# Where the sums of weight blocks are made: an accumulating DMA against VectorE and GpSimd, in a decoder trunk of seven-product matmuls

## The chip, the cores and the metric

One Trainium2 chip, one core. The metric is the device time of one execution in microseconds. DVE is VectorE, ACT ScalarE, PE TensorE (PEld its weight loads), POOL GpSimd and SP the engine that issues most of the DMAs.

## The reference

A decoder trunk of two layers on 1024 tokens of width 1024, all in float32. Layer 1 is a gated short convolution and a SwiGLU feed-forward block (FFN, hidden width 2816); layer 2 is latent attention with 8 heads and another FFN; a norm closes it.

```python
def short_conv_mixer(h, w_in, conv_w, w_out):
    u = h @ w_in                                   # 1024 -> 3 x 1024
    gate_b, gate_c, val = jnp.split(u, 3, axis=-1)
    z = gate_c * val
    conv = sum(conv_w[k] * zp[:, k:k + s] for k in range(3))   # zp: z shifted by up to 2 tokens
    return (gate_b * conv) @ w_out

def swiglu_ffn(h, w13, w2):
    g, u = jnp.split(h @ w13, 2, axis=-1)          # 1024 -> 2 x 2816
    return (jax.nn.silu(g) * u) @ w2

for i in range(2):
    h = h + (short_conv_mixer if i == 0 else mla_mixer)(rms_norm(h), ...)
    h = h + swiglu_ffn(rms_norm(h), w13[i], w2[i])
return rms_norm(h)
```

## The kernel before

**Three matmuls for one.** Every operand of a large matmul is split into a high part in the matmul's own format (`hi`, a cast on ScalarE, line 112) and the rest (`lo`, a subtraction on VectorE, line 113); `three` (lines 153 to 155) multiplies hi by hi, lo by hi and hi by lo into one bank of PSUM.

**Seven products for eight.** The matmuls into the gated layers (the `up` stages) take two blocks of 128 output columns at a time, a *quad*: the columns `ca` and `cb` of the weight, each cut into a top and a bottom half along the contraction (a0, a1, b0, b1). Instead of eight products of quarter size, seven are made, in the order 1, 2, 5, 6, 7, 4, 3. Products 1 and 2 use a0 and a1 as they are (`pair`, one split of 128x1024); 4 uses b1; 5 uses b0+b1, 6 uses a0+b0+b1, 7 uses a0+b0 and 3 uses a0+a1+b0+b1 (`half(i)`, a split of 128x512 each). One product is 12 matmuls of 128x512. `evict` adds the bank of a product into the results C1 and C2 on VectorE, in part through ScalarE, and the functions in `done` follow the last product.

**The sums.** A quad's weights lie in two tiles of 128x1024, `ra` and `rb`, from a pool of 5 buffers (`raw_tile`, named `wr` in the profile). `load` (line 363) fetches them on SP's queue. The sums are made in the tile by the DMA itself: `plus` (line 378) issues from GpSimd's queue a DMA of 256 KB that fetches a block from memory and adds it to what the tile holds. There are four per quad.

**Stages.** In order: `up` of the convolution (12 quads; three quads make two column pairs, gate_c with val, and the pair of gates for both), `Plain` (the product with w_out), `up` of FFN 1 (22 quads), `Down` of FFN 1, the latents and attention, `Plain` for the attention's output, `up` of FFN 2 (22 quads), `Down` of FFN 2 and the output. `Down` has seven products too, with weight sums of its own: `weight_sums` (line 884) has GpSimd issue DMAs, half of them from memory to memory with an addition, that leave these sums in `md["f1w"]` and `md["f2w"]` in memory. It does so during the `up` stage of the same FFN.

**The order is written out by hand.** `Steps` holds a list of TensorE steps (a product is one step); `before(n, f)` and `after(n, f)` put work ahead of step n and behind it. The program is issued in that order, so each engine's queue is in order of steps. `up` (line 446) gives the order: of the first 7 quads (FILL) products 1 and 2 come first, 14 steps; then the other five products of the first two quads in turn, then five products each of quads 2 to 6; the remaining quads run all seven. In these 49 steps products 5, 6, 7, 4 and 3 need operands that are still being prepared in the first 14 (`Operand.second`). A quad is loaded 9 or 12 steps ahead of its product 5; a `half` stands 2 steps (4 for product 5) ahead of its product.

Of the kernel before, what the change touches and what calls it, by code (L numbers as in the profile page):

```python
# [12 lines left out]
AF = mybir.ActivationFunctionType  # L13
ALU = mybir.AluOpType
AX = mybir.AxisListType

P = 128
S = 1024
D = 1024
KD = D // P  # L20
DFF = 2816
# [28 lines left out]
def trunk(ctx, tc, aps, out):  # L50
    nc = tc.nc
    A = aps
# [115 lines left out]
    for nm in ("conv_norm_g", "conv_w", "conv_ffn_norm_g", "kv_norm_g", "mla_norm_g", "kv_latent_norm_g",  # L168
               "mla_q_norm_g", "mla_ffn_norm_g", "final_norm_g"):
        a = A[nm]  # L170
        if len(a.shape) == 3:
            a = a.rearrange("a b c -> (a b c)")
        elif len(a.shape) == 2:
            a = a.rearrange("a b -> (a b)")
        n = a.shape[0] // P
# [64 lines left out]
    class Stream:  # L240


        def __init__(self):
            self.h = [None] * KD
            self.acc = None

    st = Stream()
    hd = dram.tile([KD, P, S], F32, name="hd")
    md = {"conv": dram.tile([KD, P, S], F32, name="md_conv")}
# [32 lines left out]
    class Operand:  # L282
# [16 lines left out]
        def part(self, name, kk, b):  # L299

            hi, lo = slot("xh", F32R), slot("xl", F32R)
            nc.scalar.copy(out=hi, in_=b)
            self.late.append(lambda: nc.vector.tensor_tensor(lo, b, hi.bitcast(F32), ALU.subtract))  # L303
            self.X.setdefault(name, {})[kk] = (hi, lo)
# [46 lines left out]
    class Quad:  # L351


        def __init__(self, wv, ca, cb, first, done):
            self.wv, self.ca, self.cb, self.first, self.done = wv, ca, cb, first, done
            self.W, self.bank = {}, {}

        def part(self, c, p):
            return self.wv[:, 4 * p:4 * p + 4, c:c + P]

        def load(self, c, n=8):
            r = raw_tile("wr")
            nc.sync.dma_start(r[:, :n * P].rearrange("p (k m) -> p k m", m=P), self.wv[:, :n, c:c + P])
            return r

        def load_a(self):
            self.ra = self.load(self.ca)

        def load_top(self):

            self.ra = self.load(self.ca, 4)

        def load_b(self):
            self.rb = self.load(self.cb)

        def plus(self, r, c, p):

            nc.gpsimd.dma_start(r[:, :512].rearrange("p (k m) -> p k m", m=P), self.part(c, p), accum_op=ALU.add)  # L378

        def pair(self):  # L380
            hi, lo = hi_tile("w_hi"), lo_tile("w_lo")
            split(hi, lo, self.ra)
            self.W[1], self.W[2] = (hi, lo, 0), (hi, lo, 512)

        def half(self, i):

# [55 lines left out]
    def up(steps, quads, op):  # L442

        head, n0 = quads[:FILL], len(steps.pe)
        a, b = quads[:2]
        n = {}

        for x, i in [(a, 1), (b, 1), (a, 2), (b, 2), *((x, i) for x in head[2:] for i in (1, 2)),
                     *((x, i) for i in (5, 6, 7, 4, 3) for x in (a, b)),
                     *((x, i) for x in quads[2:] for i in ((5, 6, 7, 4, 3) if x in head else (1, 2, 5, 6, 7, 4, 3)))]:  # L450
            n[x, i] = x.add(steps, op, i)
        for x in head:
            steps.before(n[x, 1] - 9, x.load_a)
            steps.before(n[x, 1] - 2, x.pair)
        for x in quads:
            n5 = n[x, 5]
            if x in head:
                steps.before(n5 - 9, x.load_top, x.load_b)
            else:
                steps.before(n5 - 12, x.load_a, x.load_b)  # L460
                steps.before(n5 - 5, x.pair)
            steps.before(n5 - 7, lambda x=x: x.plus(x.rb, x.cb, 1))
            steps.before(n5 - 4, lambda x=x: x.half(5))
            steps.before(n5 - 4, lambda x=x: x.plus(x.ra, x.cb, 0))
            steps.before(n5 - 3, lambda x=x: x.plus(x.rb, x.ca, 0))
            steps.before(n[x, 6] - 2, lambda x=x: x.half(6))
            steps.before(n[x, 6] - 1, lambda x=x: x.plus(x.rb, x.ca, 1))
            for i in (7, 4, 3):
                steps.before(n[x, i] - 2, lambda x=x, i=i: x.half(i))
        return n0  # L470

    def load_h(order):
# [224 lines left out]
    w_in = A["conv_w_in"].rearrange("a k n -> (a k) n").rearrange("(k p) n -> p k n", p=P)  # L697
# [3 lines left out]
    def conv_pair(j):  # L701
        def done(c1, c2):
            nc.vector.tensor_tensor(c1, c1, c2, ALU.mult)
            cw = lambda k: gcol("conv_w", k * KD + j)
            c = slot("conv")
            nc.vector.tensor_scalar(c, c1, cw(2), None, ALU.mult)
            for k in (1, 2):
                nc.vector.scalar_tensor_tensor(c[:, k:], c1[:, :S - k], cw(2 - k), c[:, k:], ALU.mult, ALU.add)
            kept[j] = c
        return Quad(w_in, (KD + j) * P, (2 * KD + j) * P, AF.Copy, [done])  # L710

    def gate_pair(j):
        def done(i, c):
            y = kept[i]
            nc.vector.tensor_tensor(y, y, c, ALU.mult)
            nc.sync.dma_start(md["conv"][i], y)
        return Quad(w_in, j * P, (j + 1) * P, AF.Copy, [lambda c1, c2: done(j, c1), lambda c1, c2: done(j + 1, c2)])

    conv_quads = [f(*a) for j in range(0, KD, 2) for f, a in ((conv_pair, (j,)), (conv_pair, (j + 1,)), (gate_pair, (j,)))]

    steps = Steps()
# [99 lines left out]
    def ffn_quads(w13, m):  # L821
        wv = w13.rearrange("a k n -> (a k) n").rearrange("(k p) n -> p k n", p=P)

        first = {}

        def store(i, j, t):
            nc.sync.dma_start(m[i - 1, j], t)

        def one(j):

            last, j0, box = j >= KF // 2, j % (KF // 2), {}

            def product(c1, c2):
                nc.vector.tensor_tensor(c1, c1, c2, ALU.mult)
                store(2 if last else 1, j0, c1[:, :512])
                if last:
                    store(3, j0, c1[:, 512:])
                    box["b"] = [(c[:, :512], c[:, 512:]) for c in (first.pop(j0), c1)]
                else:
                    first[j] = c1  # L840

            def left(c1, c2):
                (b11, b12), (b21, b22) = box["b"]
                box["s"] = work("msum")
                box["t1"], box["t2"] = box["s"][:, :512], box["s"][:, 512:]
                sub(5, box["t1"], b12, b11)

            def right(c1, c2):
                (b11, b12), (b21, b22) = box["b"]
                sub(6, box["t2"], b22, box["t1"])  # L850

            def low(c1, c2):
                (b11, b12), (b21, b22) = box["b"]
                sub(7, b12, b22, b12)

            def corner(c1, c2):
                (b11, b12), (b21, b22) = box["b"]
                sub(4, b21, box["t2"], b21)

            def sub(i, o, x, y):  # L860
                nc.vector.tensor_tensor(o, x, y, ALU.subtract)
                store(i, j0, o)

            done = [product, left, right, low, corner] if last else [product]
            return Quad(wv, j * P, DFF + j * P, AF.Silu, done)

        return [one(j + f) for j in range(KF // 2) for f in (0, KF // 2)]

    def weight_sums(steps, n0, w, out):

        wv, half = w.rearrange("(k p) n -> p k n", p=P), KF // 2
        n = n0 + 6
        for g in range((half + 1) // 2):
            ks = list(range(2 * g, min(2 * g + 2, half)))
            o = [out[i, g][:, :len(ks) * 512].rearrange("p (k m) -> p k m", m=512) for i in range(4)]

            def block(a, b):
                k = b * half + ks[0]
                return wv[:, k:k + len(ks), (1 - a) * 512:(2 - a) * 512]

            for i, src, add in ((0, block(1, 0), False), (3, block(0, 0), False), (0, block(1, 1), True), (3, block(1, 0), True),
                                (1, o[0], False), (1, block(0, 0), True), (2, o[1], False), (2, block(0, 1), True)):
                extra = dict(accum_op=ALU.add) if add else {}
                steps.before(n, lambda i=i, src=src, extra=extra, o=o: nc.gpsimd.dma_start(o[i], src, **extra))
                n += 3

    flat = lambda w: w.rearrange("a k n -> (a k) n")
    kp = lambda w: w.rearrange("(k p) n -> p k n", p=P)
    pairs = lambda a, b: [list(range(k, min(k + 2, b))) for k in range(a, b, 2)]
    bd = Boundary("conv_ffn_norm_g")  # L890
    n0 = len(steps.pe)
    steps.before(n0, lambda: load_h(range(KD)))
    pl = Plain(steps, kp(flat(A["conv_w_out"])), pairs(0, KD), Streamed(md["conv"], pairs(0, KD), n0), bd.norm.add)
    e = pl.ends
    bd.first(steps, e[1] + 5, (e[1] + 7, e[1] + 9, e[1] + 11, e[1] + 13))
    bd.second(steps, e[3] + 1)
    n0 = up(steps, ffn_quads(A["conv_ffn_w13"], md["f1"]), bd.op)
    weight_sums(steps, n0, flat(A["conv_ffn_w2"]), md["f1w"])


    rd = dram.tile([2, P, S], F32, name="rd")
# [77 lines left out]
    e = dn.ends  # L979
# [344 lines left out]
    e = pl.ends  # L1324
    bd.first(steps, e[1] + 4, (e[1] + 5, e[1] + 6, e[1] + 6, e[1] + 7))
    bd.second(steps, e[3] + 1)
    n0 = up(steps, ffn_quads(A["mla_ffn_w13"], md["f2"]), bd.op)
    weight_sums(steps, n0, flat(A["mla_ffn_w2"]), md["f2w"])


    fnorm = Norm()
# [73 lines left out]
```

## Time and profile before

| what | value |
|---|---|
| time, median of 3 runs | 2322.42 us (2308.9 to 2322.83) |
| the profiled execution | 2304.81 us, span 2303.0 us, mean granted clock 0.968 |
| busy share of the span | PE 93%, PEld 77%, DVE 60%, ACT 36%, POOL 22% |
| DMA queues | q1 (issued by SP) 260.35 MB, q0 (issued by GpSimd) 122.78 MB |
| `up` of the convolution, first to last matmul | 27 to 287 us |
| `up` of FFN 1 | 380 to 858 us |
| `up` of FFN 2 | 1566 to 2052 us |

A row of a group reads: line, engine, operation, output <- inputs, shapes, count | busy time in all, mean ns of one | idle time of the engine just ahead of it, and what ended most of that. A row of the waits reads: who waited <- for whom: us in total, times, the longest. Busy times of matmuls overlap, since they are pipelined: their pace is read from the starts.

### The profile page before, as it was taken

To read this page: it belongs to the slowest core of one execution; us is meant where nothing else is said; L and a number is where in the kernel's file an instruction comes from. 1 tells how busy PE (TensorE), PEld (TensorE's weight loads), DVE (VectorE), ACT (ScalarE), POOL (GpSimd) and SP (SyncE) were. 2 spreads that over 40 slices of the span, in tenths; PEclk is the share of its full clock that TensorE was granted. 3 is DMA by queue.
4 is the path that set the end of the run, shared out by engine and by line. 5 is a ranking of instruction groups with operands and counts; after the bars stand their busy time and mean duration, and the time that the engine had idled before them with its cause. 6 is when DMAs were issued, how large, how long until landed. Compare 5 with 4: busy or idle time off the path is not lost. (4 is left out here: it accounts for less than half of the span.)

```text
span 2303.0 us, 26800 instructions
## 1 busy us (share of the span) xinstructions
PE 2153.2 (93%) x9869; PEld 1765.8 (77%) x9869; DVE 1393.0 (60%) x2099; ACT 824.9 (36%) x1313; POOL 511.8 (22%) x486
## 2 busy tenths in 40 slices
PE   7989999989999999999969999999889999999997
PEld 6768788767777777788858888887667787778786
DVE  5776655755555558866247777456655556567554
ACT  6412334422332233354225545234312233333443
POOL 0332200333333320001243324100333333310000
PEclk9999999999999999999979999998999999999998
DMA  7677854699999997565022223524899999996552
GB/s 250 101 134 128 213 189 151 121 199 213 221 200 202 214 257 247 178 220 160 9 65 71 58 52 95 181 83 133 150 208 206 224 192 224 194 303 220 175 170 77
DMA packets 378866, 384.94 MB, mean 167 GB/s; under 512 B 21329, under 2 KB 286238, under 8 KB 378414
## 3 DMA queue, kind: packets, MB, share of 16 engines
q1 hardware_dynamic: 233392, 260.35, 35.1%
q0 software_dynamic: 145056, 122.78, 32.8%
q8 instruction: 77, 1.26, 0.2%
q14 instruction: 55, 0.45, 0.1%
q10 hardware_dynamic: 286, 0.11, 0.0%
HBM read 305.04 MB, written 119.01 MB: 184 GB/s over the span
## 5 line engine op out<-in xcount | busy, mean ns | idle before, releaser
L153 PE MATMUL q<-xh,w_hi 128*128 128x512 f32 x1568 | 630.3, 402 | 63.7 <-ACT w_hi L112 62.5
L155 PE MATMUL q<-xh,w_lo 128*128 128x512 f32 x1568 | 628.4, 401 | 10.0 <-DVE w_lo L113 9.7
L154 PE MATMUL q<-xl,w_hi 128*128 128x512 f32 x1568 | 624.7, 398 | 4.3 <-DVE xl L303 4.2
L113 DVE TENSOR_TENSOR w_lo<-wr,w_hi 128x1024 fp32r<-128x1024 f32 (+1 forms) x336 | 260.2, 778 | 385.6 <-ACT w_hi L112 385.1
L153 PEld LDWEIGHTS q<-xh,w_hi 128*128 128x128 f32 x1568 | 302.8, 193 | 140.1 <-ACT w_hi L112 78.0
L112 ACT CAST w_hi<-wr 128x1024 fp32r<-128x1024 f32 (+1 forms) x336 | 224.5, 688 | 486.1 <-DMA wr<-in_mla_ffn_w_dram 178.2
L155 PEld LDWEIGHTS q<-xh,w_lo 128*128 128x128 f32 x1568 | 302.4, 193 | 92.6 <-DVE w_lo L113 29.9
L154 PEld LDWEIGHTS q<-xl,w_hi 128*128 128x128 f32 x1568 | 302.7, 193 | 69.2 <-DVE xl L303 5.7
L155 PE MATMUL dn<-mp_hi,wp_lo 128*128 128x512 f32 x616 | 242.4, 394 | 6.1 <-DVE wp_lo L113 4.3
L153 PE MATMUL dn<-mp_hi,wp_hi 128*128 128x512 f32 x616 | 242.1, 393 | 0.5 <-ACT wp_hi L112 0.5
L154 PE MATMUL dn<-mp_lo,wp_hi 128*128 128x512 f32 x616 | 240.8, 391 | 1.0 <-DVE mp_lo L113 1.0
L378 POOL DMA_DIRECT2D wr<-in_conv_ffn_w_dram x88 | 118.9, 1479 | 396.1 <-DMA wr<-in_conv_ffn_w_dram 182.3
L378 POOL DMA_DIRECT2D wr<-in_mla_ffn_w_dram x88 | 119.5, 1488 | 362.6 <-DVE w_lo L113 185.4
L113 DVE TENSOR_TENSOR mp_lo<-m,mp_hi 128x1024 fp32r<-128x1024 f32 x84 | 96.6, 1150 | 128.7 <-ACT mp_hi L112 128.7
L112 ACT CAST mp_hi<-m 128x1024 fp32r<-128x1024 f32 x84 | 82.2, 979 | 214.6 <-PE dn L154 207.3
L155 PEld LDWEIGHTS dn<-mp_hi,wp_lo 128*128 128x128 f32 x616 | 115.9, 188 | 37.7 <-DVE wp_lo L113 13.9
L154 PEld LDWEIGHTS dn<-mp_lo,wp_hi 128*128 128x128 f32 x616 | 116.0, 188 | 25.7 <-DVE mp_lo L113 1.4
L153 PEld LDWEIGHTS dn<-mp_hi,wp_hi 128*128 128x128 f32 x616 | 116.0, 188 | 24.9 <-ACT wp_hi L112 1.9
L378 POOL DMA_DIRECT2D wr<-in_conv_w_in_dram x48 | 63.1, 1467 | 207.3 <-DVE w_lo L113 132.4
L406 DVE TENSOR_TENSOR c<-q,c 128x512 f32<-128x512 f32 x112 | 76.8, 686 | 38.6 <-PE q L155 36.5
L113 DVE TENSOR_TENSOR wp_lo<-w,wp_hi 128x1024 fp32r<-128x1024 f32 x84 | 94.9, 1129 | 0.0
L112 ACT CAST wp_hi<-w 128x1024 fp32r<-128x1024 f32 x84 | 82.0, 976 | 0.0
(250 smaller groups left out, 3294.9 us busy)
## 6 DMA issues: line engine op xcount, KB each, us to landing
m<-md_f SPq DMA_DIRECT2D x70, 512.0 KB, 4.8
md_f<-c SPq DMA_DIRECT2D x110, 256.0 KB, 5.9
wr<-in_conv_ffn_w_dram SPq DMA_DIRECT2D x44, 512.0 KB, 8.3
wr<-in_conv_ffn_w_dram POOLq DMA_DIRECT2D x88, 256.0 KB, 7.0
wr<-in_mla_ffn_w_dram SPq DMA_DIRECT2D x44, 512.0 KB, 7.7
wr<-in_mla_ffn_w_dram POOLq DMA_DIRECT2D x88, 256.0 KB, 6.9
w<-mw_f SPq DMA_DIRECT2D x40, 512.0 KB, 4.9
hd<-h SPq DMA_DIRECT2D x32, 512.0 KB, 3.1
```

Of the source, the lines that this page charges most:

```text
L112: nc.scalar.copy(out=hi, in_=src)
L113: (eng or nc.vector).tensor_tensor(lo, src, hi.bitcast(F32), ALU.subtract)
L153: nc.tensor.matmul(ps, lhsT=wh, rhs=xh, start=st, stop=False)
L154: nc.tensor.matmul(ps, lhsT=wh, rhs=xl, start=False, stop=False)
L155: nc.tensor.matmul(ps, lhsT=wl, rhs=xh, start=False, stop=en)
L378: nc.gpsimd.dma_start(r[:, :512].rearrange("p (k m) -> p k m", m=P), self.part(c, p), accum_op=ALU.add)
L406: add = lambda o, a: nc.vector.tensor_tensor(o, b, a, ALU.add)
```

## The change

In the `up` stages the accumulating DMAs go. Both tiles of a quad are loaded whole, and four instructions make the sums in place: `sum3` (a0+b0) and `sum1` (b0+b1), three steps ahead of product 5, `sum2` (a0+b0+b1) with `half(6)`, and `sum4` (all four) with `half(3)`. They run on VectorE; in the convolution's stage `sum3` and `sum1` run on GpSimd, four steps ahead. `half(5)` now stands two steps ahead of its product, not four. A regular quad's loads are issued 11 and 10 steps ahead of product 5 instead of 12.

In the convolution's stage the product with the first tap goes from VectorE to ScalarE.

The sums for `Down` are still made by DMA from GpSimd's queue, but a stage earlier: those of FFN 1 beside `up` of the convolution (one issue every 2 steps from step 4), those of FFN 2 beside `up` of FFN 1 (one every 3 steps). The issues are ordered by kind, all column groups of a kind after one another, where they were eight in a chain per group.

```diff
-        def __init__(self, wv, ca, cb, first, done):
+        def __init__(self, wv, ca, cb, first, done, eng):
...
-        def load_top(self):
-            self.ra = self.load(self.ca, 4)
...
-        def plus(self, r, c, p):
-            nc.gpsimd.dma_start(r[:, :512].rearrange("p (k m) -> p k m", m=P), self.part(c, p), accum_op=ALU.add)
...
+        def sum3(self):
+            self.eng.tensor_tensor(self.ra[:, :512], self.ra[:, :512], self.rb[:, :512], ALU.add)
+        def sum1(self):
+            self.eng.tensor_tensor(self.rb[:, :512], self.rb[:, :512], self.rb[:, 512:], ALU.add)
+        def sum2(self):
+            nc.vector.tensor_tensor(self.rb[:, :512], self.ra[:, :512], self.rb[:, 512:], ALU.add)
+        def sum4(self):
+            nc.vector.tensor_tensor(self.rb[:, :512], self.rb[:, :512], self.ra[:, 512:], ALU.add)
...
             if x in head:
-                steps.before(n5 - 9, x.load_top, x.load_b)
+                steps.before(n5 - 9, x.load_a, x.load_b)
             else:
-                steps.before(n5 - 12, x.load_a, x.load_b)
+                steps.before(n5 - 11, x.load_a)
+                steps.before(n5 - 10, x.load_b)
                 steps.before(n5 - 5, x.pair)
-            steps.before(n5 - 7, lambda x=x: x.plus(x.rb, x.cb, 1))
-            steps.before(n5 - 4, lambda x=x: x.half(5))
-            steps.before(n5 - 4, lambda x=x: x.plus(x.ra, x.cb, 0))
-            steps.before(n5 - 3, lambda x=x: x.plus(x.rb, x.ca, 0))
-            steps.before(n[x, 6] - 2, lambda x=x: x.half(6))
-            steps.before(n[x, 6] - 1, lambda x=x: x.plus(x.rb, x.ca, 1))
-            for i in (7, 4, 3):
-                steps.before(n[x, i] - 2, lambda x=x, i=i: x.half(i))
+            e = 0 if x.eng is nc.vector else 1
+            steps.before(n5 - 3 - e, x.sum3, x.sum1)
+            steps.before(n5 - 2, lambda x=x: x.half(5))
+            steps.before(n[x, 6] - 2, x.sum2, lambda x=x: x.half(6))
+            steps.before(n[x, 7] - 2, lambda x=x: x.half(7))
+            steps.before(n[x, 4] - 2, lambda x=x: x.half(4))
+            steps.before(n[x, 3] - 2, x.sum4, lambda x=x: x.half(3))
...
-            nc.vector.tensor_scalar(c, c1, cw(2), None, ALU.mult)
+            nc.scalar.activation(c, c1, AF.Copy, scale=cw(2))
...
+        stages = ((0, (1, 0), False), (3, (0, 0), False), (0, (1, 1), True), (3, (1, 0), True),
+                  (1, 0, False), (1, (0, 0), True), (2, 1, False), (2, (0, 1), True))
+        return [[lambda st=st, g=g: one(*st, g) for g in range(len(groups))] for st in stages]
...
+    for j, fn in enumerate(x for stage in weight_sums(flat(A["conv_ffn_w2"]), md["f1w"]) for x in stage):
+        steps.before(4 + 2 * j, fn)
...
-    weight_sums(steps, n0, flat(A["conv_ffn_w2"]), md["f1w"])
+    for j, fn in enumerate(x for stage in weight_sums(flat(A["mla_ffn_w2"]), md["f2w"]) for x in stage):
+        steps.before(n0 + 6 + 3 * j, fn)
...
-    n0 = up(steps, ffn_quads(A["mla_ffn_w13"], md["f2"]), bd.op)
-    weight_sums(steps, n0, flat(A["mla_ffn_w2"]), md["f2w"])
+    up(steps, ffn_quads(A["mla_ffn_w13"], md["f2"]), bd.op)
```

More of the change, by code (lines that the diff above doesn't have):

```diff
@@ L351, in trunk, with load @@
     class Quad:
-        def __init__(self, wv, ca, cb, first, done):
-            self.wv, self.ca, self.cb, self.first, self.done = wv, ca, cb, first, done
+        def __init__(self, wv, ca, cb, first, done, eng):
+            self.wv, self.ca, self.cb, self.first, self.done, self.eng = wv, ca, cb, first, done, eng
             self.W, self.bank = {}, {}
-        def part(self, c, p):
-            return self.wv[:, 4 * p:4 * p + 4, c:c + P]
-        def load(self, c, n=8):
+        def load(self, c):
             r = raw_tile("wr")
-            nc.sync.dma_start(r[:, :n * P].rearrange("p (k m) -> p k m", m=P), self.wv[:, :n, c:c + P])
+            nc.sync.dma_start(r.rearrange("p (k m) -> p k m", m=P), self.wv[:, :, c:c + P])
             return r
@@ L709, in done @@
             kept[j] = c
-        return Quad(w_in, (KD + j) * P, (2 * KD + j) * P, AF.Copy, [done])
+        return Quad(w_in, (KD + j) * P, (2 * KD + j) * P, AF.Copy, [done], nc.gpsimd)
     def gate_pair(j):
@@ L716, in done @@
             nc.sync.dma_start(md["conv"][i], y)
-        return Quad(w_in, j * P, (j + 1) * P, AF.Copy, [lambda c1, c2: done(j, c1), lambda c1, c2: done(j + 1, c2)])
+        return Quad(w_in, j * P, (j + 1) * P, AF.Copy, [lambda c1, c2: done(j, c1), lambda c1, c2: done(j + 1, c2)], nc.gpsimd)
     conv_quads = [f(*a) for j in range(0, KD, 2) for f, a in ((conv_pair, (j,)), (conv_pair, (j + 1,)), (gate_pair, (j,)))]
@@ L864, in one, with weight_sums @@
             done = [product, left, right, low, corner] if last else [product]
-            return Quad(wv, j * P, DFF + j * P, AF.Silu, done)
+            return Quad(wv, j * P, DFF + j * P, AF.Silu, done, nc.vector)
         return [one(j + f) for j in range(KF // 2) for f in (0, KF // 2)]
-    def weight_sums(steps, n0, w, out):
+    def weight_sums(w, out):
         wv, half = w.rearrange("(k p) n -> p k n", p=P), KF // 2
[L872 to L885, printed above, removed]
+        groups = [list(range(k, min(k + 2, half))) for k in range(0, half, 2)]
+        def one(i, src, add, g):
+            o = [out[j, g][:, :len(groups[g]) * 512].rearrange("p (k m) -> p k m", m=512) for j in range(4)]
+            if isinstance(src, tuple):
+                (a, b), k = src, groups[g][0]
+                k += b * half
+                src = wv[:, k:k + len(groups[g]), (1 - a) * 512:(2 - a) * 512]
+            else:
+                src = o[src]
+            if add:
+                nc.gpsimd.dma_start(o[i], src, accum_op=ALU.add)
+            else:
+                nc.gpsimd.dma_start(o[i], src)
+        stages = ((0, (1, 0), False), (3, (0, 0), False), (0, (1, 1), True), (3, (1, 0), True),
+                  (1, 0, False), (1, (0, 0), True), (2, 1, False), (2, (0, 1), True))
+        return [[lambda st=st, g=g: one(*st, g) for g in range(len(groups))] for st in stages]
     flat = lambda w: w.rearrange("a k n -> (a k) n")
```

## The prediction

> **What bounds the kernel now.** I read the page first: busy shares, the chain that ended last, the costliest groups.
>
> ```profile
> PE 2153.2 (93%) x9869; PEld 1765.8 (77%) x9869; DVE 1393.0 (60%) x2099; ACT 824.9 (36%) x1313; POOL 511.8 (22%) x486
> DMA wr<-in_mla_ffn_w_dram 9%; PE ps_s L1205 3%; PE dn L155 2%; PE dn L153 2%; PE dn L154 2%; PE q L153 1%; PE q L155 1%; PE q L154 1%; ACT w_hi L112 1%; DVE w_lo L113 1%; PE ps_wo L148 1%; PE ps_q L146 1%; PE ps_wo L150 1%; PE ps_wo L146 1%; PE ps_q L148 1%
> L153 PE MATMUL q<-xh,w_hi 128*128 128x512 f32 x1568 | 630.3, 402 | 63.7 <-ACT w_hi L112 62.5
> ```
>
> TensorE is the bound, but the chain's largest part that isn't TensorE is a DMA into the weight tile `wr`, and TensorE's longest idle group waits for `w_hi`, made from that tile. Both lie in the three `up` stages. How much do they lose there? The timeline gives the undisturbed pace (start, duration): the second row starts 9 matmuls after the first.
>
> ```profile
> 607.09 0.39 PE L153 MATMUL q<-xh,w_hi 128*128 128x512 f32 x1
> ...
> 609.13 0.39 PE L153 MATMUL q<-xh,w_hi 128*128 128x512 f32 x1
> ```
>
> 2.04 / 9 = 0.2265 us per matmul, 2.72 per product of 12, 19.03 per quad of seven. Next the stretch view, cut in each `up` stage (conv, FFN 1, FFN 2) where product 14 and product 49 end: start-up, the *head* (35 products of the first seven quads) and the *rest* (5 quads in conv, 15 in an FFN). Columns: stretch, length, busy time of PE, PEld, DVE, ACT, POOL, granted clock, DMA share, GB/s.
>
> ```profile
> 26.90:75.20 48.30, 47.04 (x236) 38.84 (x237) 28.18 (x35) 33.05 (x51) 7.35 (x6) 1.00 0.63 165
> 75.20:187.20 112.00, 100.75 (x415) 79.71 (x414) 83.87 (x109) 30.24 (x49) 33.32 (x26) 0.95 0.70 124
> 187.20:286.80 99.60, 97.56 (x425) 78.94 (x423) 63.65 (x82) 26.65 (x42) 23.18 (x19) 1.00 0.78 167
> 379.70:429.80 50.10, 48.15 (x214) 38.87 (x213) 30.85 (x41) 21.48 (x30) 8.99 (x8) 0.93 0.49 120
> 429.80:553.50 123.70, 107.18 (x419) 84.11 (x418) 72.67 (x104) 33.03 (x55) 43.01 (x37) 0.90 0.97 187
> 553.50:857.90 304.40, 292.85 (x1260) 236.95 (x1259) 167.87 (x237) 93.29 (x150) 102.94 (x91) 0.99 1.00 216
> 1566.30:1626.40 60.10, 53.57 (x213) 42.80 (x212) 44.46 (x59) 27.08 (x36) 8.22 (x8) 0.86 0.47 128
> 1626.40:1751.50 125.10, 106.99 (x423) 82.84 (x422) 73.38 (x105) 33.60 (x56) 44.06 (x39) 0.93 0.97 187
> 1751.50:2051.70 300.20, 291.11 (x1261) 236.31 (x1260) 168.03 (x237) 93.43 (x150) 102.58 (x91) 0.99 1.02 219
> ```
>
> At full pace a head takes 420 x 0.2265 = 95.1 us, a rest 95.1 (conv) or 15 x 19.03 = 285.5 (FFN). Excess: heads 16.9, 28.6, 30.0; rests 4.5, 18.9, 14.7. Together 113.6 us is the most that this change can reach; start-up waits on the operands' preparation, which it leaves alone. The DMA share is 0.97 to 1.02 in the FFN stretches. Last, the waits of the FFN 2 head (who waits, for whom, total, times, longest):
>
> ```profile
> ACT w_hi L112 <- DMA wr<-in_mla_ffn_w_dram: 61.3, 13, 14.3
> DVE w_lo L113 <- ACT w_hi L112: 48.4, 18, 6.6
> POOL wr L378 <- DVE w_lo L113: 40.8, 12, 8.8
> PE q L153 <- ACT w_hi L112: 17.4, 8, 5.3
> ```
>
> This is a chain: an accumulating DMA into `wr` may start only when the split has read the previous sum, the next split only when it has landed, and TensorE comes last.
>
> **What goes.** Four accumulating DMAs per quad, 224 in all.
>
> ```profile
> wr<-in_mla_ffn_w_dram SPq DMA_DIRECT2D x44, 512.0 KB, 7.7
> wr<-in_mla_ffn_w_dram POOLq DMA_DIRECT2D x88, 256.0 KB, 6.9
> L378 POOL DMA_DIRECT2D wr<-in_mla_ffn_w_dram x88 | 119.5, 1488 | 362.6 <-DVE w_lo L113 185.4 <-DMA wr<-in_mla_ffn_w_dram 137.3 <-DVE xraw L312 14.8
> ```
>
> `half(6)` and `half(3)` each come one step (2.72 us) after their accumulation is issued, two steps before their product. GpSimd's 1.5 us plus 6.9 us of landing is over 8 us against 5.4 us: late whenever nothing runs ahead. Afterwards only plain loads are awaited. A regular quad's sums come 7 and 8 steps (19 us) behind them, against 7.7 us: hidden. In a head the second load needs the buffer that quad n-2 now frees two steps later, at its `sum4`; from there to `sum3` are 5 steps, 13.6 us. It covers 7.7 us; if it didn't, VectorE itself would stand. Seven head loads grow from 256 to 512 KB and lie in that cover. SP's stores behind such a held load wait with it; their readers come a stage later.
>
> **What comes on VectorE.** Four 128x512 sums per FFN quad, two per conv quad. Same shape, from SBUF, and the spacing of such operations in a full queue:
>
> ```profile
> L861 DVE TENSOR_TENSOR c<-c,c 128x512 f32<-128x512 f32 x22 | 15.1, 685 | 0.0
> 93.69 0.68 DVE L419 TENSOR_TENSOR c<-c,q 128x512 f32<-128x512 f32 x1
> 94.28 0.69 DVE L113 TENSOR_TENSOR w_lo<-wr,w_hi 128x512 fp32r<-128x512 f32 x1
> 94.89 0.68 DVE L419 TENSOR_TENSOR c<-c,q 128x512 f32<-128x512 f32 x1
> L112 ACT CAST w_hi<-wr 128x512 fp32r<-128x512 f32 x280 | 169.8, 616 | 486.1 <-DMA wr<-in_mla_ffn_w_dram 178.2 <-DMA wr<-in_conv_ffn_w_dram 176.0 <-DMA wr<-in_conv_w_in_dram 107.5
> ```
>
> Starts lie 0.60 apart, so four cost 2.4 us. VectorE's busy time per FFN quad is 168 / 15 = 11.2 in the rest and 73.4 / 7 = 10.5 in the head. `sum2` and `sum4` are followed at once by the split of their result, so VectorE then stands through ScalarE's cast, 0.62 twice: 1.2 us, with evictions queued behind it, whose banks TensorE needs only products later. Rest: 11.2 + 2.4 + 1.2 = 14.8 of 19.0, covered. Head: 14.1 against 5 x 2.72 = 13.6, 0.5 too much per quad, 3.5 us; and six sums of the first two quads (3.6 us) fall where VectorE is still preparing operands. I put the head at 95.1 + 7 = 102 us, and leave 4 us of excess in a rest for single stalls. **FFN 1:** 28.6 - 7 + 18.9 - 4 = 36.5 saved; **FFN 2:** 30.0 - 7 + 14.7 - 4 = 33.7.
>
> **Conv.** `sum3` and `sum1` go to GpSimd, the tap product (L706) to ScalarE.
>
> ```profile
> L113 POOL TENSOR_TENSOR wv_lo<-wv_raw,wv_hi 128x512 fp32r<-128x512 f32 x4 | 5.2, 1294 | 4.9 <-ACT wv_hi L112 4.9
> L706 DVE TENSOR_SCALAR conv<-c,vec x8: 753/754/1185, 112.0 to 267.5; 128x1024 f32<-128x1024 f32 x8
> L112 ACT CAST w_hi<-wr 128x1024 fp32r<-128x1024 f32 x56 | 58.4, 1046 | 0.0
> 1090.56 2.37 POOL L113 TENSOR_TENSOR wl_lo<-wlat,wl_hi 128x1024 fp32r<-128x1024 f32 x1 [21.12 <-ACT wl_hi L112]
> 1090.62 3.38 DVE L221 TENSOR_TENSOR dg<-ident,rs 128x1024 f32<-128x1024 f32 x1
> 1204.00 2.35 POOL L113 TENSOR_TENSOR qrl<-qr,qrh 128x1024 fp32r<-128x1024 f32 x1 [0.18 <-ACT qrh L112]
> 1204.87 1.23 DVE L113 TENSOR_TENSOR qnl<-ps_q,qnh 128x1024 fp32r<-128x1024 f32 x1 [4.50 <-ACT qnh L112]
> ```
>
> A GpSimd sum lasts 1.29 us, issued four steps before its product: hidden on its own engine. The tap product leaves VectorE (0.75) but VectorE waits for it on ScalarE (1.05). The last four rows show a price: beside a GpSimd operation VectorE's sum of two SBUF operands took 3.38 us, that is the other's 2.3 us and its own 1.1; with one operand in PSUM it took 1.23, undisturbed. So 24 GpSimd sums cost VectorE between 0 and 24 x 1.29 = 31 us, 0 to 2.6 per quad; I take half, since its queue mixes both kinds. Head per quad: 83.9 / 7 = 12.0, plus 1.2 for two sums, 1.2 for casts, 2/3 x (1.05 - 0.75) = 0.2, 1.3 for the block: 15.9 against 13.6. Seven times 2.3 is 16, so 111 us where 112 are measured; the rest keeps 2.5 of its 4.5. **Conv saves 3**; 12 with no block, minus 6 with a full one.
>
> The Trainium skill, "SBUF — State Buffer", section "Who interferes with whom", calls the pair of ports that VectorE and GpSimd share an exclusive lock held for a whole instruction. By it the full 31 us would count, and conv would lose 6; the two pairs of rows agree for two SBUF operands alone.
>
> **What moves.** The sums for `down` keep their number; FFN 2's are issued in FFN 1, FFN 1's in conv, read a stage later.
>
> ```profile
> mw_f<-in_mla_ffn_w_dram POOLq DMA_DIRECT2D x30, 512.0 KB, 10.0
> L884 POOL DMA_DIRECT2D mw_f<-in_mla_ffn_w_dram x36 | 58.0, 1612 | 3.4 <-DMA mw_f<-mw_f 3.4
> ```
>
> In conv 48 issues of at most 1.6 us, 77 us, replace 48 accumulations of 1.5 on GpSimd's queue, ahead of its 24 sums (31 us): 108 of some 260 us. An addition stands at least 6 issues (12 steps, 33 us) behind the write that it needs, against 10 us: no wait ahead of a sum. All at nothing; if a sum did wait, so would `half(5)`.
>
> **The sum.** 36.5 + 33.7 + 3 = 73 us off the profiled execution's 2304.8 (span 2303.0): 2231.5. The listed runs are 2308.9 to 2322.8, median 2322.4, 4 to 18 us above; what differs between them is probably the chained waits that go, so I add 4: **2235 us**.
>
> Of the excess of the six stretches 69 us is idle TensorE (length less busy) and the remaining 45 is pace below full: the granted clock is 0.90 and 0.93 in the FFN heads. My sum returns both.
>
> **Rivals.**
> *A, VectorE binds in the heads.* If every one of the five splits waits for its cast (3.1 us a quad in place of 1.2), each FFN head is 13 us longer, and with the full block conv loses 6 instead of saving 3: 2235 + 26 + 9 = 2270. For: start-up with VectorE busy 44 of 60 us. Against: three casts need no sum just ahead and ScalarE is under a third busy. Late loads would look alike, with the DMA as releaser.
> *B, nothing takes the wait's place:* all 114 us go: 2195. Against: VectorE's 14.1 of 13.6.
> *C, slower.* VectorE's wait for the casts stays and the sums come on top. It is 48.4 / 7 = 6.9 per head quad; with 10.5 and 2.4 that is 19.8 against the 17.9 measured now, 13 us per head; if the rests keep theirs likewise, some 15 more each, 56 in both, and conv 6: 2305 + 62 = 2367. It decides once VectorE waits more than 17.9 - 12.9 = 5.0 us per head quad. Against: ScalarE's own wait for the DMA is longer (61.3) than VectorE's for ScalarE, so it is inherited.
> *D, only the idle time returns:* fewer stalls, but long enough to hold the clock down as now, so 73 x 69 / 114 = 44 us saved and 2265. Against: the clock is 0.99 in both FFN rests, where waits are shorter. The Trainium skill, "TensorE: Matmul & The Clock Gate", section "Part 1: The HAM clock gate", has the mechanism: an idle window of about 3.4 us halves the clock until a busy one has passed. The heads' waits of up to 5.3 us and their clock agree.
> *E, not what it says:* loads, not sums, were late, and the waits stay: 2305 to 2315. Against: a DMA share of 1.0 of which q0, where the accumulations are, is nearly half for under a third of the bytes.
>
> ```profile
> q1 hardware_dynamic: 233392, 260.35, 35.1%
> q0 software_dynamic: 145056, 122.78, 32.8%
> ```
>
> **How the numbers follow.** Forecast 0.55 (its own range 2212 to 2258), A 0.18, B 0.11, C 0.06, D 0.05, E 0.05. The range, 2190 to 2290, takes in the forecast, A, B, D and the block's two bounds. A measurement of this kernel tells about 1% from no change, 23 us: faster, under 2299, holds the forecast, A but for a twentieth, B and D: 0.88; slower is C, 0.06; same, E and that little of A, 0.06.
>
> **What would show it.** Right: no DMA among the releasers of `w_hi` in the heads; FFN heads near 102 us and rests near 289 at clock 0.98 or more; DMA share below 0.65 in FFN 1 and 0.5 in FFN 2; VectorE's busy time up 2.4 us per FFN quad; its two-operand operations over 1 us where a GpSimd sum runs. Wrong: VectorE waiting for a `wr` load, TensorE waiting for `w_lo` in the rests, or conv over 265 us.

## The result, and the profile after

| | before | after |
|---|---|---|
| time, median (range), number of runs | 2321.5 us (2308.9 to 2330.3), 12 | 2303.81 us (2298.05 to 2309.89), 12 |
| ratio to before | | 0.9931, interval 0.9911 to 0.9951 |
| the profiled execution, span | 2304.8, 2303.0 | 2309.9, 2308.1 |

The change brings 0.7%, where 3.7% were forecast; 2303.81 lies above the range (2190 to 2290). The ratios here and below are to runs of before that belong to the same measurement, and come with a 95% interval; they aren't exactly the quotients of the medians. The profiled execution of before was the shortest of its runs and that of after the longest, so their spans differ by 5 us in the other direction; stages are compared below, not spans.

The page of after: its busy shares, its queues, the chain that ended last (by engine), and the group that was quoted for before:

```profile
PE 2152.8 (93%) x9869; PEld 1770.5 (77%) x9869; DVE 1525.6 (66%) x2291; ACT 833.6 (36%) x1321; POOL 249.7 (11%) x286
q1 hardware_dynamic: 244144, 265.86, 35.1%
q0 software_dynamic: 26784, 64.04, 11.3%
PE 36%; DVE 5%; ACT 2%; issue 2%; DMA 1%; POOL 0%; SPq 0%; ACTq 0%; DVEq 0%; POOLq 0%
L153 PE MATMUL q<-xh,w_hi 128*128 128x512 f32 x1568 | 623.6, 398 | 28.7 <-ACT w_hi L112 27.3
```

What was meant has happened: q0 fell from 122.78 to 64.04 MB and from 32.8% to 11.3%, the DMAs' share of the chain that ended last fell from 10% to 1%, and TensorE's idle time at L153 in the `up` stages went from 63.7 to 28.7 us. The stretch view of after, cut at the same matmuls as before: conv (start-up, head, rest), then Plain in one piece, FFN 1 and FFN 2 (three each). Columns: stretch, length, busy PE, PEld, DVE, ACT, POOL, granted clock, DMA share, GB/s.

```profile
28.10:76.20 48.10, 46.45 (x233) 38.03 (x233) 30.08 (x35) 33.36 (x50) 9.15 (x9) 1.00 0.63 194
76.20:196.30 120.10, 105.81 (x421) 83.00 (x422) 94.91 (x117) 34.34 (x53) 32.63 (x28) 0.93 0.58 142
196.30:291.60 95.30, 95.30 (x422) 78.51 (x421) 71.47 (x90) 29.64 (x45) 33.12 (x37) 1.00 0.68 176
291.60:430.80 139.20, 97.20 (x404) 78.65 (x402) 54.48 (x65) 35.10 (x41) 35.86 (x45) 0.83 1.07 298
430.80:493.00 62.20, 51.30 (x212) 40.16 (x210) 35.05 (x46) 23.64 (x32) 0.00 (x0) 0.89 0.53 154
493.00:599.00 106.00, 101.54 (x421) 78.45 (x422) 86.00 (x126) 32.53 (x54) 0.00 (x0) 0.98 0.32 99
599.00:885.50 286.50, 286.40 (x1261) 236.03 (x1260) 211.23 (x303) 93.21 (x151) 0.00 (x0) 1.00 0.37 119
1604.10:1664.80 60.70, 52.86 (x212) 41.87 (x211) 46.20 (x61) 27.88 (x37) 0.00 (x0) 0.86 0.39 121
1664.80:1770.80 106.00, 101.32 (x420) 78.29 (x421) 85.89 (x125) 32.49 (x54) 0.00 (x0) 0.98 0.31 100
1770.80:2057.50 286.70, 286.62 (x1262) 236.22 (x1261) 211.34 (x304) 93.20 (x151) 0.00 (x0) 1.00 0.37 119
```

The FFN heads are 106.0 us (124 before) and the rests 286.5 (304 and 300): the rests stand at TensorE's full pace (285.5 by the matmuls' starts). The loss is the fourth row. The same stretch of before, Plain from its first matmul to FFN 1's first:

```profile
286.70:379.10 92.40, 90.70 (x403) 74.02 (x402) 58.46 (x72) 34.67 (x42) 0.00 (x0) 1.00 0.53 175
```

Plain grew from 92.4 to 139.2 us, with the same matmuls, at a DMA share of 1.07 and with GpSimd, idle there before, issuing 45 DMAs. Against before the profiled stages changed by +3.8 (conv), **+46.8 (Plain)**, -24.0 (FFN 1, whose start-up alone became some 12 longer), -31.7 (FFN 2) and +10.2 (all others): +5.1, the difference of the spans.

Why does GpSimd work in Plain? Its timeline in before, the only row between 272.6 and 420 us (start, duration, in brackets how long the engine had been idle and for whom):

```profile
404.48 1.30 POOL L378 DMA_DIRECT2D wr<-in_conv_ffn_w_dram  x1 [130.60 <-DMA wr<-in_conv_ffn_w_dram]
```

and in after, from conv's last sum on:

```profile
270.16 1.63 POOL L380 TENSOR_TENSOR wr<-wr 128x512 f32<-128x512 f32 x1
271.72 3.03 POOL L889 DMA_DIRECT2D mw_f<-mw_f  x6
...
285.61 1.75 POOL L889 DMA_DIRECT2D mw_f<-in_mla_ffn_w_dram  x2
...
417.05 3.99 POOL L887 DMA_DIRECT2D mw_f<-in_mla_ffn_w_dram  x4 [0.31 <-DMA mw_f<-mw_f]
```

In before, the weight sums of FFN 1 stood in GpSimd's queue behind an accumulation into `wr`, which waited 130.6 us for that tile's load. This wait tied the queue to the time of the stage. In after, nothing of FFN 1 but the weight sums is on the queue: FFN 2's are all issued between 285 and 421 us, before FFN 1's first matmul at 430.8, though the order written out by hand puts them beside FFN 1's products. A place in the order is a place in an engine's queue, not a time. What they hit, by the waits of after in Plain:

```profile
POOL mw_f L889 <- DMA mw_f<-in_mla_ffn_w_dram: 44.2, 16, 3.6
ACT mh L112 <- DMA m<-md_conv: 40.3, 1, 40.3
PE pl L153 <- ACT mh L112: 37.4, 1, 37.4
```

ScalarE waits 40.3 us for one load of Plain's left operand, and TensorE stands for 37.4 of them. (In before ScalarE waited 13.2 us there, and TensorE lost nothing by it.) TensorE's granted clock falls with that, as three stretches of 10 us show:

```profile
300.00:310.00 10.00, 8.36 (x36) 6.26 (x34) 3.59 (x3) 3.00 (x3) 1.84 (x3) 1.00 1.07 326
310.00:320.00 10.00, 0.00 (x0) 0.00 (x0) 0.00 (x0) 0.00 (x0) 2.50 (x5) 0.62 1.03 420
320.00:330.00 10.00, 0.00 (x0) 0.00 (x0) 0.00 (x0) 0.00 (x0) 4.16 (x4) 0.50 1.02 379
```

### The profile page after: what moved, and what is told of

It is laid out like the page before. It is cut to its first block, busy times and chain, and to the rows that moved or that the text cites. A ratio compares the mean times of both kernels' runs of the same rounds, so it can differ in the third digit from the quotient of the medians.

```text
span 2308.1 us, 26314 instructions
## 1 busy us (share of the span) xinstructions
PE 2152.8 (93%) x9869; PEld 1770.5 (77%) x9869; DVE 1525.6 (66%) x2291; ACT 833.6 (36%) x1321; POOL 249.7 (11%) x286
## 3 DMA queue, kind: packets, MB, share of 16 engines
q0 software_dynamic: 26784, 64.04, 11.3%
## 5 line engine op out<-in xcount | busy, mean ns | idle before, releaser
L153 PE MATMUL q<-xh,w_hi 128*128 128x512 f32 x1568 | 623.6, 398 | 28.7 <-ACT w_hi L112 27.3
L153 PEld LDWEIGHTS q<-xh,w_hi 128*128 128x128 f32 x1568 | 299.6, 191 | 100.6 <-ACT w_hi L112 38.8
L155 PEld LDWEIGHTS q<-xh,w_lo 128*128 128x128 f32 x1568 | 299.2, 191 | 91.1 <-DVE w_lo L113 28.8
L153 PE MATMUL dn<-mp_hi,wp_hi 128*128 128x512 f32 x616 | 242.1, 393 | 0.5 <-ACT wp_hi L112 0.5
L153 PEld LDWEIGHTS dn<-mp_hi,wp_hi 128*128 128x128 f32 x616 | 116.0, 188 | 24.8 <-ACT wp_hi L112 1.9
L431 ACT ACTIVATE c<-c 128x512 f32<-128x512 f32 x44 | 27.8, 633 | 209.7 <-DVE c L409 209.7
L153 PE MATMUL pl<-mh,wp_hi 128*128 128x512 f32 x128 | 52.5, 410 | 37.4 <-ACT mh L112 37.4
L1014 POOL TENSOR_TENSOR wlat<-wlat,vec 128x1024 f32<-128x1024 f32 (+1 forms) x4 | 7.8, 1943 | 671.6 <-DMA wlat<-in_mla_w_dq_dram 671.6
```

The lines of the kernel that those rows point to most:

```text
L153: nc.tensor.matmul(ps, lhsT=wh, rhs=xh, start=st, stop=False)
L155: nc.tensor.matmul(ps, lhsT=wl, rhs=xh, start=False, stop=en)
L431: nc.scalar.activation(self.C1[:, 512:], self.C1[:, 512:], self.first)
```

## The experiments

Three theories of the growth between conv and FFN 1 were to be told apart: the queue runs ahead (1), the amount of DMA moved (2), or what conv itself leaves behind, its stores and FFN 1's weight sums (3). The stage times below run from a stage's first matmul to the next one's, in the profiled execution; *head* is the 35 products of the first seven quads.

**A brake on the queue.** A small GpSimd instruction that reads the quad's tile `ra` stands two steps ahead of product 5 of every quad of FFN 1, and for the first seven quads ahead of product 1 too: 29 in all, of 0.19 to 1.29 us. Nothing else is changed.

```diff
+        def tick(self):
+            o = small.tile([P, 1], F32, name="tick", bufs=4)
+            nc.gpsimd.tensor_tensor(o, self.ra[:, 0:1], self.ra[:, 1:2], ALU.add)
...
             steps.before(n[x, 1] - 2, x.pair)
+            if tick:
+                steps.before(n[x, 1] - 2, x.tick)
...
             steps.before(n5 - 2, lambda x=x: x.half(5))
+            if tick:
+                steps.before(n5 - 2, x.tick)
...
-    n0 = up(steps, ffn_quads(A["conv_ffn_w13"], md["f1"]), bd.op)
+    n0 = up(steps, ffn_quads(A["conv_ffn_w13"], md["f1"]), bd.op, True)
```

> The changed kernel plus a GpSimd addition of one column per quad of FFN 1's up stage that reads the quad's weight tile, so that GpSimd's queue can't pass the steps. Theory 1 (with no work of its own in FFN 1, GpSimd's queue runs ahead of the written order and issues FFN 2's weight sums as soon as the convolution's last sum is made; they fill the DMA engines while Plain loads): Plain, from its first matmul to FFN 1's first, falls from 139 us to 93 to 97, FFN 1's start-up loses some 10 us of waiting, and the whole is 2240 to 2262. Theory 2 (it is the amount of DMA, wherever it stands): what Plain regains FFN 1's loads lose, 2290 to 2310. Theory 3 (the convolution's own late stores and FFN 1's weight sums hold Plain up): Plain stays at 130 to 140 and the whole at 2300 to 2308.

Measured: 2269.58 us, ratio 0.9797 (0.9771 to 0.9824). GpSimd's timeline shows the brake: its first instruction waits through most of Plain (289.9 to 400.3 us here) for FFN 1's first load, and the first of FFN 2's sums comes at 399 us, not at 285:

```profile
369.83 0.19 POOL L390 TENSOR_TENSOR tick<-wr 128x1 f32<-128x1 f32 x1 [85.08 <-DMA wr<-in_conv_ffn_w_dram]
...
399.12 0.71 POOL L897 DMA_DIRECT2D mw_f<-in_mla_ffn_w_dram  x1 [0.28 <-issue]
```

Plain fell from 139.2 to 110.4 us and FFN 1 from 454.7 to 444.9. The three stretches of FFN 1 with the 48 weight sums now beside it:

```profile
400.30:451.80 51.50, 47.84 (x212) 38.29 (x210) 32.14 (x43) 22.05 (x30) 3.48 (x5) 0.93 0.46 142
451.80:558.60 106.80, 101.97 (x421) 78.66 (x422) 86.03 (x126) 32.54 (x54) 11.51 (x18) 0.98 0.52 153
558.60:845.20 286.60, 286.45 (x1262) 236.15 (x1261) 211.14 (x303) 93.01 (x151) 37.39 (x48) 1.00 0.65 174
```

The amount of DMA is that of after, so theory 2 falls: some 31 to 34 us of after's time (by the ratios and by the medians) were the missing brake. Theory 1 is right in kind but promised too much: Plain didn't come back to 93 to 97 us, nor the whole to 2262. The DMA share in FFN 1 is at or under the bound that the prediction gave, 0.65.

**No weight sums for FFN 2 at all** (the `steps.before` of that loop is left out; this leaves out FFN 2's weight sums, and its `Down` reads FFN 1's).

> The changed kernel without FFN 2's weight sums (48 DMAs left out; Down of FFN 2 reads FFN 1's in their place), to see what they cost in all. Theories 1 and 2: Plain 93 to 97 and 2240 to 2260; by theory 1 within 8 us of the run with GpSimd held to the steps, by theory 2 at least 30 below it. Theory 3: Plain stays above 130, over 2290.

Measured: 2265.34 us, ratio 0.9779 (0.9752 to 0.9805); Plain 109.9, FFN 1 443.9. That is 4 us below the braked version, as theory 1 has it, and not 30. The stages say that even these 4 aren't the price of the sums: FFN 1 differs by 1.0 us and Plain by 0.5, while conv, which is the same in both, differs by 2.6. With a brake, FFN 2's sums cost about 1 us beside FFN 1. But 17 us of Plain's growth remain, and FFN 2's sums have no part in them.

**FFN 1's weight sums out of conv as well**, both sets beside FFN 1, braked:

```diff
-    for j, fn in enumerate(... "conv_ffn_w2" ...): steps.before(4 + 2 * j, fn)
-        steps.before(n0 + 6 + 3 * j, fn)                # FFN 2's
+        steps.before(n0 + 78 + 3 * j // 2, fn)
+    for j, fn in enumerate(... "conv_ffn_w2" ...): steps.before(n0 + 4 + 3 * j // 2, fn)
```

> The ticked version with FFN 1's weight sums also moved, from the conv stage into FFN 1's own up stage (two a step from its start; FFN 2's two a step from the middle), so that none is issued in conv or beside Plain. Theory 3a (the 17 us that Plain still has over before, 110 against 92, are FFN 1's 48 sums issued in a burst behind conv's last sum): conv 257 to 262, Plain 92 to 96, FFN 1's up 446 to 452, in all about 2254, some 15 below the ticked version. Rival (FFN 1's up stage has no room for twice as many sums at its start, its head is late): Plain as before, but FFN 1's up at 460 or more, in all 2265 to 2275. Second rival (the 17 us come from something else, such as conv's own stores): Plain stays near 110.

Measured: 2253.32 us, ratio 0.9728 (0.9691 to 0.9766). Conv 257.8, Plain 91.7 (before 92.4), FFN 1 448.2: the 17 us were FFN 1's sums. In after the last 12 of the 48 stand in the queue behind conv's last sum, and GpSimd issued them in a burst from 271.7 us on (second row of after's timeline above). By the written order, one every 2 steps from step 4, the last eight of them belong beside Plain anyway, since conv ends at step 84. The head and rest of FFN 1, with 96 weight sums beside them:

```profile
428.30:538.60 110.30, 103.74 (x421) 79.63 (x422) 86.29 (x126) 32.67 (x54) 21.86 (x30) 0.97 0.75 200
538.60:825.10 286.50, 286.35 (x1260) 235.99 (x1260) 211.14 (x303) 92.97 (x151) 63.89 (x81) 1.00 0.88 230
```

At a DMA share of 0.88 the rest is still at full pace; the head pays some 4 us against after's 106.0.

**One half of the change alone: the weight sums moved, the chains kept.** `weight_sums` and its two loops as in after, all else as in before.

> The kernel before, with only the weight sums for Down moved one stage ahead and ordered by kind. Theory 1: the accumulating DMAs of the quads hold GpSimd's queue to the steps, so Plain stays at 93 to 100; FFN 2 gains 10 to 25 us from fewer DMAs, the convolution loses 5 to 15; 2300 to 2325. Theory 2: the same total, since the DMA work is the same; 2315 to 2325. Theory 3: Plain 125 or more and 2340 or more.

Measured: 2320.68 us, ratio 1.0031 (1.001 to 1.0053). The total fits theories 1 and 2 alike; the trace tells them apart. The old chain in FFN 1 is a brake as theory 1 has it, and all but one of FFN 2's sums stay out of Plain:

```profile
449.16 1.33 POOL L378 DMA_DIRECT2D wr<-in_conv_ffn_w_dram  x1 [132.52 <-DMA wr<-in_conv_ffn_w_dram]
```

Plain took 107.8 us, though, not 93 to 100: with FFN 1's sums in conv, 15 us are lost here, much as in the braked version. Conv became 285.0 (259.7 before), more than was expected: accumulations and weight sums share GpSimd's queue, and the DMA share is 0.94 to 1.03 from product 15 on. FFN 1, with chains and 48 weight sums as before, took 479.2 (478.7). But FFN 2's `up`, with the old chains and no weight sums beside it, took 454.0 (head 105.0, rest 288.9), where before it was 485.1 and with sums on VectorE 453.4. The landing times say why; the DMA view of FFN 2's rest (here all but its first and last few us) in before and in this version (KB each, median us from issue to landing):

```profile
wr<-in_mla_ffn_w_dram POOLq DMA_DIRECT2D x57, 256.0 KB, 6.6
wr<-in_mla_ffn_w_dram SPq DMA_DIRECT2D x26, 512.0 KB, 8.0
```

```profile
wr<-in_mla_ffn_w_dram POOLq DMA_DIRECT2D x57, 256.0 KB, 4.7
wr<-in_mla_ffn_w_dram SPq DMA_DIRECT2D x26, 512.0 KB, 5.2
```

The chain of four accumulations was late because the DMA engines were full. With the weight sums gone, the DMA share of the rest is 0.80, not 1.02, each accumulation lands 1.9 us sooner and the chain keeps up. GpSimd is also rid of 49 us of other issues in that stretch, and no run takes these away alone; but 57 landings that are 1.9 us shorter, 108 us, cover the 84 us by which ScalarE's waits for transfers into `wr` fell (116.9 to 33.4). So this half of the change alone frees FFN 2. That the other half does so too is shown in FFN 1 only: with sums on VectorE it took 444.9 with 48 weight sums beside it and 448.2 with 96.

**The other half alone: the sums on VectorE, the weight sums in their old places.**

> The sums of a quad on VectorE and GpSimd as in the changed kernel, but the weight sums for Down left in the stage of their own FFN, in chains per group, as before. Theory 1: the FFN 1 sums are issued early just as well, so Plain takes 120 to 140 us, and FFN 2's run ahead into the attention's end; 2300 to 2340. Theory 2: FFN 1 and FFN 2 near 455 each with Plain at 93, 2250 to 2265. Theory 3: Plain back at 93 because the convolution has no weight sums beside it, 2250 to 2265.

Measured: 2296.81 us, ratio 0.9916 (0.9887 to 0.9945). This run didn't test what it was to test. FFN 2 has a list of steps of its own, issued behind the attention; with no accumulation left in it, its weight sums came to stand at the front of GpSimd's queue (the first was issued at 1.95 us), so the queue isn't in the written order across the two lists. Why, no run shows. Conv took 295.9 us. The waits from 78 to 250 us, its head and a little around it, show what a sum behind a waiting DMA issue costs:

```profile
POOL mw_f L887 <- DMA mw_f<-in_mla_ffn_w_dram: 62.1, 13, 9.1
ACT w_hi L112 <- POOL wr L380: 47.8, 5, 26.7
PE q L153 <- ACT w_hi L112: 36.7, 9, 21.9
```

GpSimd waits for a transfer before it may issue an addition, the sum behind it waits too, ScalarE waits for the sum (up to 26.7 us), and TensorE stands for 36.7 us in nine waits for ScalarE.

FFN 1's 48 sums ran ahead as theory 1 expected, from 309 us on, and half of them were issued before FFN 1's first matmul at 428.9; its `up` took 447.6. But Plain took 99.8 us, not the 120 to 140 of theory 1. In chains per group most issues wait for an earlier one to land: 20 were issued in Plain, where after has 45. So a queue that runs ahead isn't enough to cost 47 us; the new order by kind, which lets the issues follow each other closely, seems to have a part in it, which no run here separates.

**Conv's GpSimd sums on VectorE**, and **the tap's product back on VectorE**, each against the version with both sets in FFN 1:

```diff
-        return Quad(w_in, ..., nc.gpsimd)
+        return Quad(w_in, ..., nc.vector)
```

> As the version with both sets of sums in FFN 1, and conv's weight sums that were on GpSimd put on VectorE. Lock theory (two-operand VectorE instructions of conv are long because they stand beside GpSimd's sums, which costs the head of conv its time): conv's head from about 116 to about 108. Load theory (the head is bound by the amount of work on VectorE): the head grows, to 122 or more, and conv to 268 or more. In all 2246 by the first, 2262 or more by the second.

```diff
-            nc.scalar.activation(c, c1, AF.Copy, scale=cw(2))
+            nc.vector.tensor_scalar(c, c1, cw(2), None, ALU.mult)
```

> As the version with both sets of sums in FFN 1, and the tap's product of conv, which the change put elsewhere, back on VectorE. Lock theory: nothing gained, conv within 1 us or up to 2 us better, GpSimd or ScalarE being less laden. Load theory: conv's head about 3 us longer. In all within 4 us of that version either way.

Measured: 2248.19 us, ratio 0.9717 (0.9681 to 0.9753), conv 259.7 with a head of 115.0; and 2247.21 us, ratio 0.9707 (0.9677 to 0.9737), conv 257.1 with a head of 114.2. The version that they are held against had 257.8 and 113.6. All three are the same within their intervals; the first fits neither of its two theories, and in the second conv's head is 0.6 us longer, not the 3 of the load theory. The 5 and 6 us between the medians needn't be the change's either: the profiled executions differ by as much in the stage with the attention (504.3, 496.5 and 496.4 us), which is the same in all three. Why conv's head stays as it was, the groups by shape in it say, with the sums on GpSimd:

```profile
L113 DVE TENSOR_TENSOR w_lo<-wr,w_hi 128x512 fp32r<-128x512 f32 x35 | 27.1, 775 | 14.0 <-ACT w_hi L112 13.9
L714 DVE TENSOR_TENSOR c<-c,c 128x1024 f32<-128x1024 f32 x4 | 6.0, 1488 | 0.0
L429 DVE TENSOR_TENSOR c<-c 128x512 f32<-128x512 f32 x7 | 5.4, 777 | 0.2
L719 DVE SCALAR_TENSOR_TENSOR conv<-c,vec,conv 128x1023 f32<-128x1023 f32 x4 | 5.1, 1284 | 4.9 <-ACT conv L717 4.9
L380 POOL TENSOR_TENSOR wr<-wr 128x512 f32<-128x512 f32 x6 | 9.4, 1563 | 0.5
L377 POOL TENSOR_TENSOR wr<-wr 128x512 f32<-128x512 f32 x6 | 8.4, 1400 | 102.3 <-DVE w_lo L113 60.4 <-DMA wr<-in_conv_w_in_dram 29.9 <-DVE wr L383 9.9
```

and on VectorE:

```profile
L113 DVE TENSOR_TENSOR w_lo<-wr,w_hi 128x512 fp32r<-128x512 f32 x35 | 24.1, 689 | 11.3 <-ACT w_hi L112 11.3
L714 DVE TENSOR_TENSOR c<-c,c 128x1024 f32<-128x1024 f32 x4 | 4.9, 1219 | 0.0
L429 DVE TENSOR_TENSOR c<-c 128x512 f32<-128x512 f32 x7 | 4.8, 692 | 0.2
L380 DVE TENSOR_TENSOR wr<-wr 128x512 f32<-128x512 f32 x6 | 4.2, 692 | 0.2
L377 DVE TENSOR_TENSOR wr<-wr 128x512 f32<-128x512 f32 x6 | 4.1, 684 | 0.0
```

Beside 17.8 us of GpSimd sums VectorE's work on two operands in SBUF is 3.0 + 1.1 + 0.6 = 4.7 us longer; to do those sums itself costs it 8.3, less 2.7 us of waiting for casts that it no longer has. The two nearly cancel. The same holds for the tap: on VectorE, where its row in the same view is

```profile
L717 DVE TENSOR_SCALAR conv<-c,vec 128x1024 f32<-128x1024 f32 x4 | 3.0, 753 | 0.1
```

it costs 3.0 us, and the 4.9 us of waiting for ScalarE at L719 go.

## Why the prediction was wrong

**What moves, "All at nothing": this step failed, and it decides the result.** The step counted the issues that GpSimd gets in conv and the distance from an addition to the write that it needs. It did not ask what would hold FFN 2's sums back once no accumulation is left in FFN 1's part of the queue. The trace of before had the answer, in the row of 130.6 us. By the runs: the missing brake cost some 34 us of the median (28.8 in Plain and 9.8 in FFN 1 by the profiled executions), and FFN 1's sums in conv 16 more (2269.6 to 2253.3; by the profiled executions 18.7 in Plain and 4.3 in conv, less 3.3 in FFN 1). The 33 us between dependent additions failed for the same reason, steps taken for times: behind conv's last sum six issues went out in 3.03 us, and the next waited for a landing. No sum in conv waited for one, as forecast. Of the 69 us between 2235 and the measured time these two make 50. Of the rest, 9 are sizes (below), and about as much is the start of the sum: it set out from 2309, where the medians of before are 2313 to 2322.

**What goes, "late whenever nothing runs ahead": the reading was wrong, though its sum came out.** 1.5 + 6.9 us against 5.4 was taken as a property of the chain. With 4.7 us to land, 6.2 against 5.4 still looks late, and yet the chained rest took 288.9 us. The 6.9 us was the price of full DMA engines. This didn't hurt the forecast, because the change removes both causes, but it would have misled anyone who wanted one of them alone.

**What comes on VectorE: held, in part by luck.** Forecast heads of 102 and rests of 289.5; measured 106.0 and 286.5, so that two misses nearly cancel. In FFN 2, which nothing else disturbs, 31.7 us were saved where 33.7 were forecast. Most of the marks held too: clocks of 0.98 and 1.00, DMA shares of 0.32 to 0.53 and 0.31 to 0.39, and no DMA where `w_hi` is waited for. The first two waits of FFN 1's head in after (the others of `w_hi` are for VectorE's sums too):

```profile
ACT w_hi L112 <- DVE wr L386: 28.7, 7, 8.2
DVE w_lo L113 <- ACT w_hi L112: 19.1, 23, 1.6
```

VectorE does bind in the heads, as rival A had it: in FFN 1's it is busy for 86.0 us and waits 19.1 us for casts, together 105.1 of 106.0. That wait is 2.7 us per quad, where the forecast had 1.2 and A 3.1. But VectorE's busy time rose by 1.9 per quad of this head, not 2.4, as part of the sums fell into start-up, and so the head is 4 us beyond the forecast, a third of A's 13. In a rest VectorE's busy time per quad rose by (211.2 - 168) / 15 = 2.9 us, not 2.4: four durations of 0.685, 2.7 us, were to be added and not four spacings.

**Conv: mis-sized, in both directions.** Forecast 257, measured 263.5 in after, and 257 to 260 without the weight sums beside it. The block was put at half of GpSimd's time and measured as 4.7 of 17.8 us, about a quarter. In the trace with the sums on GpSimd, 28 of the head's 35 `w_lo` subtractions run clear of a GpSimd sum and take 0.69 us; the seven that run beside one take 1.12 on average, while evictions with an operand in PSUM keep their 0.68 beside one. The Trainium skill, "SBUF — State Buffer", section "Who interferes with whom", draws the line there: a VectorE instruction with two SBUF inputs contends with a GpSimd instruction that reads SBUF, one with at most one SBUF input doesn't. The trace agrees, so the prediction's "by it the full 31 us would count" took more from that section than it says. What was too low is the wait for casts, 8.4 us by 1.2 for each of seven quads in the head: the row of `w_lo` has 14.0, and L719 another 4.9. The heads with FFN 1's sums beside them took 120.1 us in after, 118.8 with the brake and 116.3 without FFN 2's sums, though these three have the same conv; what makes the difference is open.

**The sum.** With the queue held and conv's burst gone, the three versions stand 64, 69 and 70 us below the runs of before on their chip (2317.0), where the sum had 73. By stages the first of them has 1.9 us in conv, 30.5 in FFN 1 and 32.0 in FFN 2, 64 where the forecast had 3, 36.5 and 33.7. So the sizes were nearly right, for sums that stay where the order puts them; in after they didn't. Of the rivals, A was right in kind; B and D were not seen (heads at 106, but at a clock of 0.98); E named the right resource, full DMA engines, but not what follows from it. C, the slower one, had no part. None of the rivals was the one that came: work that leaves its stage.

**Open:** between FFN 1's `Down` and FFN 2's first matmul, code that no version touches, the profiled executions differ. Before, the version with both sets in FFN 1, and that with the tap on VectorE:

```profile
1075.50:1566.40 490.90, 457.21 (x2583) 396.67 (x2582) 277.98 (x610) 191.01 (x404) 133.77 (x160) 0.97 0.28 82
```

```profile
1041.50:1545.80 504.30, 472.31 (x2583) 409.48 (x2582) 279.07 (x610) 190.97 (x404) 133.31 (x160) 0.94 0.28 80
```

```profile
1039.90:1536.30 496.40, 462.59 (x2583) 401.47 (x2582) 279.19 (x610) 190.97 (x404) 133.64 (x160) 0.96 0.28 81
```

The same work takes 491 to 504 us as the granted clock goes from 0.97 to 0.94. All nine profiled executions lie in that range, 492.7 us with the sums alone on VectorE and 496.6 with the weight sums alone moved, so neither half of the change shows in it. No run here separates chance from a cause.

## What to carry to other kernels

Before removing instructions from a queue, look in the trace for what waits behind them: a wait that looks like a loss may be the only thing that keeps later, independent transfers in their stage. If it goes, put a cheap instruction with the right dependence in its place. And when a chain of transfers is late, read its landing times at a lower DMA share before blaming its length: here taking other traffic away was worth as much in FFN 2 as taking the chain apart too (454.0 and 453.4 us).

## What the runs showed that was not expected

- In after, DMA issues that depend on nothing in their stage ran as far ahead as their queue let them: 48 were issued from 285 to 421 us, all before the first matmul of the stage beside which they were placed. In the braked version 29 small GpSimd instructions hold them, at a cost of about 1 us in FFN 1.
- At a DMA share of 0.88 sums on VectorE kept TensorE at full pace (286.5 us in a rest), while chained accumulations at about 1.0 lost 15 to 19 us there.
- Sums on GpSimd and two-operand work in SBUF on VectorE lengthen each other: in conv's head 1.29 us became 1.40 and 1.56 on GpSimd, and 0.69 became 0.78 on VectorE, on average.
